# Attention of a diffusion trunk: softmax, weight splits and modulation products in a written order, scale in the queries, one weight queue, gate rows in steps

## The chip, the cores and the metric

The kernel runs on one core of a Trainium2 chip. The metric is the device time of one execution in microseconds, as the median of several runs; lower is better. One further execution is recorded by the profiler, and its rows are what is quoted as the profile and the trace.

Five engines take part. TensorE (PE; its weight loads are listed apart as PEld) multiplies and transposes, VectorE (DVE) and ScalarE (ACT) do the elementwise work and the reductions, GpSimd (POOL) issues a few transfers, and SyncE (SP) issues most of them.

## The reference

One layer on 640 tokens (512 latent, 128 context), D = 1024: a SwiGLU half step, a token mixer, a second half step, each with a normalisation whose shift, scale and gate come from a conditioning vector (`adaln`, nine vectors of 1024 columns). The token mixer projects to ten pieces, runs differential attention beside an mLSTM, gates both and projects back. What the change touches is the attention, the gates of the mLSTM and the modulation columns:

```python
def adaln(cvec, w, b):
    m = jax.nn.silu(cvec) @ w + b
    return m.reshape(cvec.shape[0], N_MOD, D_MODEL)
...
    mq, mk, mv, mo, mg, dq, dk, dv, gm, gd = split_cols(h @ p['w_in'][l])
    dq = rmsnorm(dq.reshape(B, T, DA_HEADS, 2, DA_HEAD_DIM), p['g_qn'][l])
    dk = rmsnorm(dk.reshape(B, T, DA_HEADS, 2, DA_HEAD_DIM), p['g_kn'][l])
...
    # latent tokens: q_att = rope_2d(dq), keys = rope_2d(dk) and 256 cached keys
    scale = DA_HEAD_DIM ** -0.5                      # 64 ** -0.5 = 0.125
    s = jnp.einsum('bqhcd,bkhcd->bhcqk', qi, kf) * scale
    pr = jax.nn.softmax(s, axis=-1)
    w = pr[:, :, 0] - lam * pr[:, :, 1]
    return jnp.einsum('bhqk,bkhv->bqhv', w, vf)
...
    gates = (mg + p['b_gate'][l]) ...
    log_i = gates[:, 0]
    log_f = jax.nn.log_sigmoid(gates[:, 1])          # then running sums and maxima by chunks of 128
```

There are 8 attention heads with two score maps each, over 512 + 256 keys for a latent query and 128 keys for a context query.

## The kernel before

All matmuls of the weights are done with operands split into a high and a low part (`split_w`: ACT copies the raw weights to the high part, DVE subtracts it from the raw weights to give the low part), three products each (`mm3`). Raw weights come into a ring of two buffers (`rawp`, 1 MB each), split weights go to a ring of two (`wp`).

The stage in question is the attention, from line 1464 to line 1670. TensorE's order is written out: every matmul and transpose is kept in program order (`mm`, `tr`). The instructions of DVE, ACT and SP are ordered by the scheduler, from a simulated timeline, unless they pass through `placed` while `as_written` is set or are issued under `issue_after`.

Two streams are woven into each other on TensorE.

- The attention itself, head by head (`Head`, line 1333). A head takes five steps `qi` of 128 queries (four latent, one context). `scores(qi)` makes the score maps of both components (`sc` in PSUM, one buffer), takes the row maxima `mx` on DVE, multiplies them by -0.125 to `nm`, takes two exponentials on ACT with that bias and the scale 0.125 and their row sums `sm`, and mixes the two on DVE: reciprocal `rc`, factor `r`, and the product-sum `p0` (line 1417; the trace names it `p<-p,r,p`). `turn(qi)` transposes `p0` on TensorE (`ps_wT`) and copies the first four blocks to `wT` on ACT, the last two on DVE (line 1432). `values(qi)` multiplies by the values (`ps_o`) and scales by `rc` into `ao`. In the head loop (line 1596) step `qi` does `scores(qi)`, `turn(qi - 1)`, some fill, `values(qi - 1)`, some fill. At `qi == 3` the queries and keys of the next head are packed (`pack`); behind the fifth step they are transposed (`queries`, `keys`, PSUM tile `ps_qkT`).
- The fill (`Fill`, line 1076): the projections by `w_mq`, `w_mk`, `w_dq`, `w_dk`, `w_mv`, `w_dv`, `w_mo`, `w_gm`, `w_gd`, a granule of 256 output columns each, cut into four feature units (`ps_p`, 24 matmuls of 320 columns) or five token units (`ps_t`, 24 matmuls of 256 columns). `slot` runs units as a pace in microseconds asks for. `one` splits the weights of the granule in front and of the one behind it. A granule of `w_dq` or `w_dk` can be held back by `ready` until the last reader of the old queries or keys has been issued. Its last unit is followed by `qk_norm_rope`: normalisation and rotation of 640 tokens, mostly on DVE.

Beside these the stage holds `gate_rows` (line 1176), some 35 small DVE and ACT instructions on the gate logits, written before the first scores; and 14 of the modulation's column products (`Columns.tile`, line 695): a load of 512 KB (`raw_a`), which takes a buffer of the raw weight ring, and two DVE products with a sum (`L704`), in heads 1 to 5. The pools of the mLSTM's queries and keys (`mlq`, `mlk`) are opened before the head loop, when the pool of the gate rows is closed.

Of the kernel before, what the change touches and what calls it, by code (L numbers as in the profile page):

```python
# [7 lines left out]
F32 = mybir.dt.float32  # L8
# [23 lines left out]
def tile_trunk(ctx: ExitStack, tc: tile.TileContext, a: dict):  # L32
# [23 lines left out]


# [74 lines left out]
    def split_into(h, lo, src):  # L132
        raw = load_raw(src)
        act(h, raw, AF.Copy)
        tt(vec, lo, raw, h.bitcast(F32), ALU.subtract)
        return h, lo

    def split_w(src, pool=None, tag="w"):
# [3 lines left out]
        return split_into(h, lo, src)  # L142
# [535 lines left out]
    class Columns:  # L678
# [16 lines left out]
        def tile(self, behind=None):  # L695
# [4 lines left out]
            with ExitStack() as st:  # L700
                if behind is not None:
                    st.enter_context(tc.issue_after(behind.ins))
                for v in range(2):
                    vec.tensor_tensor_reduce(  # L704
                        out=junk, in0=raw, in1=self.csil[:, v, :], op0=ALU.mult, op1=ALU.add, scale=1.0, scalar=0.0,
                        accum_out=mod[:, ct, v : v + 1],
                    )
# [368 lines left out]
    class Fill:  # L1076


        def __init__(self):
            self.q = []  # L1080
            self.due = self.rate = 0.0

        def granule(self, src, units, ready=lambda: True):

            self.q.append([src, units, None, ready])

        def prefetch(self, i):
            if i < len(self.q) and self.q[i][2] is None:
                self.q[i][2] = split_w(self.q[i][0])

        def one(self):
# [4 lines left out]
            self.prefetch(1)  # L1096
# [9 lines left out]
        def blocked(self):  # L1106
            return not self.q or not self.q[0][3]()
# [4 lines left out]
        def slot(self, least=1, weight=1.0):  # L1112
            self.due += self.rate * weight
            while not self.blocked() and (least > 0 or self.due > 1.4):
                self.one()
                least -= 1

        def begin(self, src, units):

            i = 0  # L1120
            while i < len(self.q) and self.q[i][2] is not None:
                i += 1
            w = split_w(src)
            return [lambda u=u: u[1](w) for u in units]
# [51 lines left out]
    def gate_rows(gt, ps):  # L1176
# [16 lines left out]
        stt(lf, fg, 0.0, e, ALU.min, ALU.subtract)  # L1193
# [3 lines left out]
        vec.memset(b, 0.0)  # L1197
        vec.tensor_tensor_scan(out=b[0:4], data0=keep[0:4], data1=lf[0:4], initial=0.0, op0=ALU.mult, op1=ALU.add)
        vec.tensor_tensor_scan(out=b[32:36, ::-1], data0=keep[32:36, ::-1], data1=lf[32:36, ::-1], initial=0.0, op0=ALU.mult, op1=ALU.add)
        tt(vec, u, ig, b, ALU.subtract)  # L1200
# [5 lines left out]
        vec.memset(M, 0.0)  # L1206
        for d0, fl in ((0, False), (32, True)):
            r = slice(d0, d0 + 4)
            for c0, c1, init in ((0, 512, m0[r, 0:1]), (512, 640, 0.0)):
# [3 lines left out]
                vec.tensor_tensor_scan(out=v(M), data0=v(A), data1=v(u), initial=init, op0=ALU.add, op1=ALU.max)  # L1213
        Ml, bl, mn, MP, dc = (gt.tile([64, 5], F32, name=n) for n in ("Ml", "bl", "mn", "MP", "dc"))
# [18 lines left out]

        QA = gt.tile([128, T], F32, name="QA")
# [98 lines left out]
    class Head:  # L1333
# [53 lines left out]
        def scores(self, qi):  # L1387
# [18 lines left out]
            w = 768 if qi < 4 else 128  # L1406
            mx, nm, sm, rc = (ap.tile([128, 2], F32, tag=n, name=n, bufs=2) for n in ("mx", "nm", "sm", "rc"))
            r = ap.tile([128, 1], F32, tag="r", name="r", bufs=2)
            vec.tensor_reduce(out=mx, in_=sv, axis=AX.X, op=ALU.max)
# [7 lines left out]
            stt(p0[:, :w], p1[:, :w], r, p0[:, :w], ALU.mult, ALU.add)  # L1417
            self.s[qi] = (p0, rc)

        def turn(self, qi):  # L1420
# [3 lines left out]
            for k0 in range(0, nk, 4):  # L1424
# [4 lines left out]
                if k0 == 0:  # L1429
                    act(wT[:, :n, :], p[:, :n, :], AF.Copy)  # L1430
                else:
                    vec.tensor_copy(wT[:, k0 : k0 + n, :], p[:, :n, :])
# [48 lines left out]
    g_q, g_k = (load(ap, [128, 64], a[n].partition_broadcast(128), name=n) for n in ("g_qn", "g_kn"))  # L1481
    with tc.issue_after(box["normed"]):
# [54 lines left out]
    with gates:  # L1537
        src_v, e_v = project_v(0)
# [611 lines left out]
```

## Time and profile before

| | us |
|---|---|
| median of 3 runs | 1858.63 |
| lowest and highest | 1857.59, 1860.19 |
| the profiled execution, its own time | 1856.65 |
| its span, first to last instruction | 1854.9 |
| mean granted TensorE clock | 0.994 |

The page lists the busy time of each engine as a share of the span, and groups of instructions as `line engine operation out<-in shape xcount | busy us, mean ns of one | idle time before it and what ended it`. In a list of waits, a row is `who waited <- for whom: us in total, times, longest us`. A line such as L59, L43, L46, L49 or L53 is that of a helper (`mm`, `act`, `tt`, `stt`, `ts`), so groups are told apart by their tiles.

### The profile page before, as it was taken

The numbers are of one execution on the slowest core, as the hardware profiler recorded it, in microseconds if no ns is written. First come the engines' busy times: TensorE is split into PE (matmuls) and PEld (weight loads), VectorE is DVE, ScalarE is ACT, GpSimd is POOL, SyncE is SP. The second block draws the span as 40 slices with busy tenths as digits, with TensorE's granted clock in tenths as the row PEclk, the third lists the DMA queues.
The fourth block names the chain that finished last, engine by engine and source line by source line (L and its number), as shares of the span: only waits on it lengthen the run. The fifth ranks groups of instructions, "written<-read, shape, count | busy, mean of one in ns | idle before, by whom it ended". The sixth has DMA issues, their size and how long they took to land.

```text
span 1854.9 us, 30739 instructions
## 1 busy us (share of the span) xinstructions
PE 1810.4 (98%) x12678; PEld 1771.0 (95%) x12678; DVE 1299.3 (70%) x2181; ACT 834.7 (45%) x1419; POOL 30.9 (2%) x55
## 2 busy tenths in 40 slices
PE   7999999999999999999999999999999999999999
PEld 5999999999999999999999999899999999999999
DVE  5889886586885665765755547874456878887575
ACT  4654544112554353543454346565235645554232
POOL 0000001010000000000000000000000000000000
PEclk9999999999999999999999999999999999999999
DMA  7364457963414322322222254656442345447872
GB/s 288 118 226 161 165 193 277 362 222 132 136 64 130 124 75 95 117 82 96 99 80 75 84 177 144 187 203 215 168 138 94 126 154 177 168 171 258 316 285 85
DMA packets 127901, 299.82 MB, mean 162 GB/s; under 512 B 9553, under 2 KB 90705, under 8 KB 114961
## 3 DMA queue, kind: packets, MB, share of 16 engines
q1 hardware_dynamic: 118498, 257.49, 40.4%
q0 software_dynamic: 9264, 40.37, 5.9%
q8 instruction: 99, 1.62, 0.4%
q14 instruction: 40, 0.33, 0.1%
HBM read 234.20 MB, written 63.63 MB: 161 GB/s over the span
## 4 chain that ended last, share of the span: by engine, by line
PE 83%; DVE 7%; DMA 6%; ACT 2%; issue 1%; SPq 0%; DVEq 0%; ACTq 0%
PE ps_f L59 39%; PE ps_p L59 21%; PE ps_t L59 12%; PE sc L59 2%; PE ps_o L59 2%; DMA ada<-csil_dram 1%; DVE ww L46 1%; PE ps_n L59 1%; PE ps_qkT L62 1%; PE ps_wT L62 1%; DMA raw_a<-in_w_ada_c 1%; DMA raw<-in_w2b 1%; PE ps_u L59 1%; DMA a_raw<-aT_dram 1%; DMA hm<-g_dram 1%
## 5 line engine op out<-in xcount | busy, mean ns | idle before, releaser
L59 PE MATMUL ps_f<-S,ww 128*128 128x320 f32 x1956 | 315.3, 310 | 5.8 <-DVE ww L46 4.0
L59 PEld LDWEIGHTS ps_f<-S,ww 128*128 128x128 f32 x1956 | 294.0, 188 | 8.5 <-DVE ww L46 6.9
L59 PE MATMUL ps_p<-hH,wH 128*128 128x320 f32 x864 | 273.5, 317 | 1.1 <-DVE y L46 0.7
L59 PE MATMUL ps_p<-hH,wL 128*128 128x320 f32 x864 | 267.1, 309 | 0.0
L59 PE MATMUL ps_p<-hL,wH 128*128 128x320 f32 x864 | 267.0, 309 | 0.0
L59 PE MATMUL ps_f<-hm,ww 128*128 128x320 f32 x1236 | 195.0, 310 | 1.5 <-DVE ww L46 1.1
L59 PEld LDWEIGHTS ps_f<-hm,ww 128*128 128x128 f32 x1236 | 185.1, 188 | 2.3 <-DVE ww L46 1.3
L59 PE MATMUL ps_t<-wH,hH 128*128 128x256 f32 x640 | 186.3, 291 | 1.0 <-DVE x L49 1.0
L59 PE MATMUL ps_t<-wH,hL 128*128 128x256 f32 x640 | 182.6, 285 | 0.0
L43 ACT ACTIVATE ww<-raw 128x2048 fp32r<-128x2048 f32 (+1 forms) x61 | 114.1, 1870 | 152.1 <-PE ps_f L59 104.0
L59 PE MATMUL ps_t<-wL,hH 128*128 128x256 f32 x640 | 182.2, 285 | 0.0
L59 PEld LDWEIGHTS ps_p<-hH,wH 128*128 128x128 f32 x864 | 162.4, 188 | 2.5 <-issue 0.9
L59 PEld LDWEIGHTS ps_p<-hL,wH 128*128 128x128 f32 x864 | 162.5, 188 | 0.5
L59 PEld LDWEIGHTS ps_p<-hH,wL 128*128 128x128 f32 x864 | 162.2, 188 | 0.0
L59 PE MATMUL ps_f<-hm,wB 128*128 128x320 f32 x984 | 157.7, 309 | 0.0
L46 DVE TENSOR_TENSOR ww<-raw,ww 128x2048 fp32r<-128x2048 f32 (+1 forms) x61 | 136.4, 2235 | 30.2 <-ACT ww L43 30.2
L59 PEld LDWEIGHTS ps_f<-hm,wB 128*128 128x128 f32 x984 | 147.7, 188 | 0.0
L46 DVE TENSOR_TENSOR wL<-raw,wH 128x2048 fp32r<-128x2048 f32 x49 | 112.1, 2288 | 38.9 <-ACT wH L43 38.8
L43 ACT ACTIVATE wH<-raw 128x2048 fp32r<-128x2048 f32 (+1 forms) x57 | 98.1, 1728 | 88.1 <-PE ps_p L59 83.5
L59 PEld LDWEIGHTS ps_t<-wH,hH 128*128 128x128 f32 x640 | 123.9, 194 | 2.0 <-issue 1.2
L59 PEld LDWEIGHTS ps_t<-wH,hL 128*128 128x128 f32 x640 | 123.8, 193 | 0.5 <-DVE hL L49 0.5
L59 PEld LDWEIGHTS ps_t<-wL,hH 128*128 128x128 f32 x640 | 123.9, 194 | 0.2
(295 smaller groups left out, 3226.7 us busy)
## 6 DMA issues: line engine op xcount, KB each, us to landing
g_dram<-g SPq DMA_DIRECT2D x44, 640.0 KB, 5.5
raw_a<-in_w_ada_c SPq DMA_DIRECT2D x24, 512.0 KB, 4.4
raw<-in_w1b SPq DMA_DIRECT2D x11, 1024.0 KB, 4.8
raw<-in_w3b SPq DMA_DIRECT2D x11, 1024.0 KB, 5.0
raw<-in_w1a SPq DMA_DIRECT2D x10, 1024.0 KB, 4.8
raw<-in_w3a SPq DMA_DIRECT2D x10, 1024.0 KB, 6.1
ada<-in_w_ada_c POOLq DMA_DIRECT2D x18, 512.0 KB, 5.1
hm<-g_dram POOLq DMA_DIRECT2D x7, 1280.0 KB, 10.7
```

The lines of the kernel that those rows point to most:

```text
L43: return placed(nc.scalar.activation(*args, **kw))
L46: return placed(eng.tensor_tensor(out=out, in0=in0, in1=in1, op=op))
L59: tc.keep_in_program_order(nc.tensor.matmul(*args, **kw))
L62: tc.keep_in_program_order(nc.tensor.transpose(*args, **kw))
```

## The change

- **A written order.** A new context `written()` chains the DVE instructions issued under it, and the ACT instructions likewise, to one another in program order, without a semaphore. Instructions outside it are still placed by the scheduler, between or around the chain. Under it stand the reduction of the scores, `turn`, the exponentials (now `soft`), the mix (now a method of its own, after the first fill of the step), `values`, `pack`, the column products in heads 1 to 3 and the splits of `ahead`.
- **The scale.** `g_q` is multiplied by -0.125 once. The row reduction is then a minimum `mn`, used as the bias directly, with the scale -1 in the exponential; `nm` and its product are gone.
- **The transposed weights.** Both copies of `wT` are made by ACT.
- **One weight queue.** All granules are listed at the start, in a fixed order; `w_dq` and `w_dk` of the second pair stand before the first `w_mk`. How many units run at each place is in the table `UNITS`; `ready`, `begin` and the pace are not used in this stage. `ahead()`, at the end of each step, splits the two granules in front and loads the raw weights of the third; `one` splits only the granule in front, if that has not been done.
- **Modulation columns.** The 14 products stand in heads 0 (two) to 3 (four in each of heads 1, 2 and 3). Their loads go to tiles of the `mlq` and `mlk` pools, opened in the third step of head 0 by `begin_pools`.
- **Gate rows.** `gate_rows` is a generator in six pieces; the first runs before head 0, the others over its first three steps (`ROWS`).

```diff
     def placed(ins):
-        if as_written[0]:
+        if as_written[0] is in_row:
+            i = ins.ins
+            if i.engine in in_row:
+                tc.add_manual_dep(
+                    i, in_row[i.engine].name, mybir.DependencyInfo(mybir.DependencyClass.NoSync, mybir.DependencyReason.DATA),
+                    reason="written",
+                )
+            in_row[i.engine] = i
+        elif as_written[0]:
             tc.keep_in_program_order(ins)
         return ins
...
+        def ahead(self):
+            for i in range(2):
+                self.prefetch(i)
+            if len(self.q) > 2 and self.q[2][3] is None:
+                self.q[2][3] = load_raw(self.q[2][0])
...
             self.prefetch(0)
-            self.prefetch(1)
+            if self.eager:
+                self.prefetch(1)
...
-            vec.tensor_reduce(out=mx, in_=sv, axis=AX.X, op=ALU.max)
-            ts(nm, mx, -0.125, ALU.mult)
+            placed(vec.tensor_reduce(out=mn, in_=sv, axis=AX.X, op=ALU.min))
...
+        def soft(self, qi):
...
-                act(p[:, :w], sv[:, c, :], AF.Exp, bias=nm[:, c : c + 1], scale=0.125, accum_out=sm[:, c : c + 1])
-            vec.reciprocal(rc, sm)
+                self.exp = act(p[:, :w], sv[:, c, :], AF.Exp, bias=mn[:, c : c + 1], scale=-1.0, accum_out=sm[:, c : c + 1])
...
+        def mix(self, qi):
+            p0, p1, w, sm, rc = self.s[qi]
+            r = ap.tile([128, 1], F32, tag="r", name="r", bufs=2)
+            placed(vec.reciprocal(rc, sm))
             stt(r, sm[:, 0:1], nlam, rc[:, 1:2], ALU.mult, ALU.mult)
...
-                if k0 == 0:
-                    act(wT[:, :n, :], p[:, :n, :], AF.Copy)
-                else:
-                    vec.tensor_copy(wT[:, k0 : k0 + n, :], p[:, :n, :])
+                act(wT[:, k0 : k0 + n, :], p[:, :n, :], AF.Copy)
...
+    ts(g_q, g_q, -0.125, ALU.mult)
...
+    def begin_pools():
+        gates.close()
+        in_pools["k"] = ctx.enter_context(tc.tile_pool(name="mlk", bufs=1, side="right"))
+        in_pools["q"] = queries_of.enter_context(tc.tile_pool(name="mlq", bufs=1, side="right"))
+        csil = Two(in_pools[t].tile([128, D], F32, tag=t + "3", name="csil") for t in "qk")
+        for v in range(2):
+            nc.sync.dma_start(out=csil[:, v, :], in_=csil_dram[v].partition_broadcast(128))
+        columns.place(14, csil, load_columns, 1)
...
     def load_columns(src):
+        t, junk = (in_pools[p].tile([128, 2, T], F32, tag=p + "2", name="raw_a").rearrange("p a b -> p (a b)") for p in "qk")
+        dma(t[:, :D], src)
+        return t[:, :D], junk[:, : D // 2].bitcast(BF16)
...
+    for pr in range(4):
+        feature(a["w_mq"][pr], lambda pr=pr: q_evac(pr))
+        if pr == 0:
+            token(project_q(1))
+            token(project_k(1))
+        feature(a["w_mk"][pr], lambda pr=pr: k_evac(pr))
+        if pr in (1, 2):
+            token(project_q(pr + 1))
+            token(project_k(pr + 1))
+        rest(pr)
+        if pr < 3:
+            token(project_v(pr + 1))
...
+    ROWS = {(0, 0): 1, (1, 0): 1, (1, 1): 1, (2, 0): 2}
+
+    def aside(hd, qi, part):
+        if hd == 0:
+            for _ in range(ROWS.get((qi, part), 0)):
+                next(rows, None)
+        if part == 0 and (hd in (1, 2, 3) and qi > 0 or hd == 0 and qi > 2):
+            with written():
+                columns.tile()
...
+    UNITS = {
+        0: ((2, 1), (1, 1), (1, 2), (2, 2), (2, 0), (2, 1, 1)), 1: ((2, 1), (1, 1), (1, 1), (1, 1), (1, 0), (1,)),
+        2: ((2, 1), (1, 1), (1, 1), (1, 1), (1, 1), (1, 1, 1)), 3: ((2, 2), (1, 1), (1, 1), (1, 1), (1, 1), (1,)),
+    }
+    UNITS.update({4: UNITS[2], 5: UNITS[3], 6: ((2, 1), (1, 1), (1, 1), (1, 1), (1, 0), (1, 1, 1)), 7: ((2, 1), (1, 1), (1, 1), (1, 0), (1, 0))})
...
         for qi in range(5):
-            if hd or qi:
+            n = UNITS[hd][qi]
+            with written():
                 H.scores(qi)
-            if hd in range(1, 6) and qi in (1, 3) or hd in range(1, 5) and qi == 2:
-                columns.tile()
-            if qi > 0:
-                H.turn(qi - 1)
-            if hd == 1 and qi in (2, 3):
-                gate_cols()
-            fill.slot()
+                if qi > 0:
+                    H.turn(qi - 1)
+                H.soft(qi)
+            aside(hd, qi, 0)
+            fill.units(n[0])
+            with written():
+                H.mix(qi)
...
             if qi > 0:
-                H.values(qi - 1)
+                with written():
+                    H.values(qi - 1)
             if qi == 3 and hd < 7:
-                heads[hd + 1].pack()
-                state["packed"] = hd + 1
-            if qi < 4:
-                fill.slot()
+                with written():
+                    heads[hd + 1].pack()
+            aside(hd, qi, 1)
+            if (hd, qi) == (0, 2):
+                begin_pools()
+            fill.units(n[1])
+            with written():
+                fill.ahead()
```

More of the change, by code (lines that the diff above doesn't have):

```diff
@@ L1 @@
[L1 removed]
+from contextlib import ExitStack, contextmanager
 import concourse.bass as bass
@@ new lines, in tile_trunk @@
+    feature(a["w_gd"][1], lambda: gate_evac(mp, gd_dram, 1))
+    fill.units(2)
+    heads[0].pack_keys()
+    heads[0].queries()
+    fill.units(3)
+    heads[0].keys(0)
+    fill.units(1)
+    heads[0].keys(1)
+    with tc.issue_after(heads[0].at_vec.ins), tc.issue_after(heads[0].at_act.ins):
+        rows = gate_rows(gt, ps_g)
+        next(rows)
+    fill.units(1)
+    fill.eager = False
+    ROWS = {(0, 0): 1, (1, 0): 1, (1, 1): 1, (2, 0): 2}
[6 more added lines that the diff above has]
+                columns.tile()
+        if part == 1 and hd == 1 and qi in (1, 2):
+            gate_load(qi - 1)
+        if part == 0 and hd == 1 and qi in (2, 3):
+            gate_cols()
@@ L1830, in tile_trunk @@
     in_order[0] = False
-    columns.place(10, csil2, load_columns, 1)
-    fill.one()
-    fill.one()
+    columns.place(10, csil2, load_columns_raw, 1)
+    with written():
+        fill.units(2)
     for i in range(5):
```

181 lines of the change are left out of this document (82 added, 99 removed).

## The prediction

> **What bounds the kernel now.** I read the page first, then the table by stretches, then what TensorE waited for, then the chain of waits through one step of the attention.
>
> ```profile
> span 1854.9 us, 30739 instructions
> ...
> PE 1810.4 (98%) x12678; PEld 1771.0 (95%) x12678; DVE 1299.3 (70%) x2181; ACT 834.7 (45%) x1419; POOL 30.9 (2%) x55
> ```
>
> TensorE (PE) is busy for 98% of the span, so nothing but its idle time, and the time in which its clock is down, can be gained: the change leaves every matmul and transpose in place. The edited stage runs from the first score product at 541 us to the last at 1083 us. The next fence is the table by stretches (columns: stretch, its length, busy time of PE, PEld, DVE, ACT and POOL with instruction counts, granted clock, DMA share, GB/s).
>
> ```profile
> 541.00:1083.00 542.00, 530.12 (x4078) 520.99 (x4077) 345.47 (x568) 241.49 (x468) 0.00 (x0) 1.00 0.29 96
> 541.00:618.00 77.00, 72.30 (x514) 70.52 (x513) 51.69 (x92) 30.40 (x59) 0.00 (x0) 1.00 0.37 120
> 533.00:536.40 3.40, 3.40 (x19) 3.40 (x18) 3.25 (x9) 2.84 (x5) 0.00 (x0) 0.50 0.00 0
> 672.90:676.30 3.40, 3.40 (x22) 3.40 (x20) 1.98 (x3) 2.63 (x5) 0.00 (x0) 0.51 0.02 5
> ```
>
> PE idles 542 - 530.1 = 11.9 us in the stage, and in two stretches of 3.4 us its clock is at half, which loses 1.7 us each. DVE (345 of 542, 64%) and ACT (45%) have room on average. So the stage is bound by PE, broken by a few waits. These are the waits of the weight loads from 520 to 1083 us, and the one wait of PE itself that lies ahead of 541:
>
> ```profile
> PEld ps_wT L62 <- DVE p L49: 7.6, 6, 2.2
> PEld ps_o L59 <- DVE wT L1432: 3.2, 2, 2.2
> PEld ps_qkT L62 <- issue: 2.7, 1, 2.7
> PEld ps_qkT L62 <- ACT kpk L43: 1.9, 1, 1.9
> ```
> ```profile
> PE ps_qkT L62 <- ACT kpk L43: 1.7, 1, 1.7
> ```
>
> Ten waits, 7.6 + 3.2 + 2.7 + 1.9 = 15.4 us by the weight loads; by PE's own idle time 11.9 + 1.7 = 13.6. I take the middle, 14.5.
>
> **How a wait comes about.** DVE from 838 to 847 us, and the transpose that it held up:
>
> ```profile
> 838.06 2.28 DVE L46 TENSOR_TENSOR wL<-raw,wH 128x2048 fp32r<-128x2048 f32 x1
> 840.25 0.16 DVE L53 TENSOR_SCALAR nm<-mx 128x2 f32<-128x2 f32 x1
> ...
> 844.91 1.23 DVE L704 CUSTOM_DVE_ANT_0 raw_a<-raw_a,csil 128x1024 bf16<-128x1024 f32 x1 [1.41 <-DMA raw_a<-in_w_ada_c]
> ...
> 846.07 1.01 DVE L49 SCALAR_TENSOR_TENSOR p<-p,r,p 128x768 f32<-128x768 f32 x1
> ```
> ```profile
> 847.14 0.55 PE L62 MATMUL ps_wT<-ident,p 128*128 128x128 f32 x3 [1.81 <-DVE p L49]
> ```
>
> Between the maximum and its tiny product nm the scheduler put a weight split (2.28), so the exponentials, which need nm, started that much late. Then a modulation product, itself waiting 1.41 for its DMA, went ahead of the mix of the two softmaxes (line 1417), and the transposes waited 1.81 for that. The work was not too much; its order was wrong.
>
> **The change, part by part.** First the cover of one step, from the chain in order of time, and a feature unit from elsewhere in the chain (columns: start, us, what):
>
> ```profile
> 627.51 1.41 PE sc L59 x8
> 628.92 0.66 PE ps_wT L62 x6
> 629.58 2.87 PE ps_t L59 x24
> 632.45 1.34 PE ps_o L59 x12
> ```
> ```profile
> 710.00 3.52 PE ps_p L59 x24
> ```
>
> From the end of one score product PE has the transposes of the step before (0.66), a unit, the values (1.34), a second unit and the next scores (1.41) to do before it needs the mix: 0.66 + 2.87 + 1.34 + 2.87 + 1.41 = 9.15 us with token units, 10.45 with feature units. What must fit in comes from the groups of instructions of the stage (count | busy us, mean ns of one | idle before):
>
> ```profile
> L46 DVE TENSOR_TENSOR wL<-raw,wH 128x2048 fp32r<-128x2048 f32 x28 | 64.0, 2287 | 12.6 <-ACT wH L43 12.5
> L1409 DVE TENSOR_REDUCE mx<-sc 128x2 f32<-128x1536 f32 x32 | 56.2, 1756 | 40.1 <-PE sc L59 40.0
> L704 DVE CUSTOM_DVE_ANT_0 raw_a<-raw_a,csil 128x1024 bf16<-128x1024 f32 x28 | 34.2, 1223 | 20.6 <-DMA raw_a<-in_w_ada_c 15.0 <-DMA csil<-csil_dram 5.4
> L49 DVE SCALAR_TENSOR_TENSOR p<-p,r,p 128x768 f32<-128x768 f32 x32 | 32.6, 1017 | 0.9
> L1432 DVE COPY wT<-ps_wT 128x256 f32<-128x256 f32 x32 | 13.3, 416 | 0.1
> L49 DVE SCALAR_TENSOR_TENSOR r<-sm,nlam,rc 128x1 f32<-128x1 f32 x40 | 8.8, 219 | 1.1
> L53 DVE TENSOR_SCALAR nm<-mx 128x2 f32<-128x2 f32 x40 | 6.5, 162 | 0.3
> L1272 DVE TENSOR_REDUCE ss<-sq 128x20 f32<-128x1280 f32 x6 | 8.9, 1479 | 0.0
> ```
> ```profile
> L43 ACT ACTIVATE p<-sc,nm 128x768 f32<-128x768 f32 x64 | 57.1, 900 | 37.0 <-DVE nm L53 32.4 <-DVE bl L1216 4.6
> L43 ACT ACTIVATE wH<-raw 128x2048 fp32r<-128x2048 f32 x27 | 51.6, 1911 | 42.0 <-PE ps_p L59 42.0
> L43 ACT ACTIVATE stage<-ps_t 128x256 f32<-128x256 f32 x20 | 7.7, 383 | 22.6 <-PE ps_t L59 22.1 <-ACT p L43 0.5
> ```
>
> *Scale folded.* The 40 nm products go (6.5 us of DVE). The reduction becomes a minimum of the same shape, so 1.76 as before, and nothing can stand between it and the exponentials any more. The one new product, on 64 columns of g_q, has no reason to differ from a small DVE product; beside matmuls I price it at 0.
>
> *Transposed weights.* The 32 second copies leave DVE (13.3 us) for ACT, at 0.383 each by a copy of the same size out of PSUM: 12.3 us more on ACT, 47% instead of 45%. They follow the first copy at once and have a unit of PE work for cover. The two waits of ps_o for wT on DVE (3.2) go; what is late next is the first copy, already on ACT.
>
> *Written order.* Reduction 1.76, two exponentials 1.80, then reciprocal (about 0.16, as nm), r 0.22, mix 1.02: 5.0 us against 9.15. With a modulation pair behind the reduction (2 x 1.22) the exponentials run beside it: 1.76 + 2.45 + 1.40 = 5.6, slack 3.5. The worst place is a split whose buffer has only just come free: ACT half 1.91, then DVE half 2.29 ahead of the reduction. That ends 4.2 us after the unit instead of the 1.41 of the scores, 2.8 later: 8.4 of 9.15. It still fits, by under 1 us, once each in heads 3 and 5. Splits elsewhere come a unit or more after their buffer is free. So the six waits for p (7.6) should go.
>
> *Projection order.* The granules for heads 2 and 3 move ahead of the keys of the first mLSTM head, so the rotation of q_tok ends about a granule earlier (4 x 3.52 = 14 us), and the wait of 2.7 at 672 us goes, with the half clock behind it (1.7). One more unit (2.87) ahead of the first key transposes covers the 1.9 of kpk; the other half clock (1.7) goes with it. Gain of the clock: 3.4.
>
> A rule weighed: the Trainium skill, page "TensorE: Matmul & The Clock Gate", section "What's actually happening", says that the clock halves after an idle window of about 3.4 us. By that page neither wait here would do it, and the sum would be 3.4 us smaller. The trace disagrees with a full window as the condition: half-clock stretches follow waits of 1.7 and 2.7 us. But it also shows 1.00 over 541 to 618 us, where PE idled 77 - 72.3 = 4.7 us, so not each wait brings one.
>
> *Gate rows and columns.* The same DVE work, in five pieces over head 0, where up to two units stand on either side. The modulation products move from heads 1 to 5 into heads 0 to 3, into memory that comes free when the gate rows have left by DMA in the third step; the weight ring no longer shares its two buffers with them. I allow 1 us of new wait there (bounds 0 and 3).
>
> *What is left or new.* The rotations are not in the written chain: six sets with a reduction of 1.48 and several passes like it can still slip in ahead of a reduction or mix. With a slack of 3.5 in the usual step one passes free; in the tight steps it shows. Bounds 0 and 6 x 2 passes x 1 us = 12, and I take 3, a quarter. One more for steps with a single unit. Sum of new waits 1 + 3 + 1 = 5, bounds 0 and 15.
>
> Sum: -14.5 - 3.4 + 5 = -12.9 us. The profiled execution took 1856.65 (span 1854.9), 1.98 below the median 1858.63 of the three runs; on the median the forecast is 1845.7.
>
> **Rivals.**
>
> *The written order waits for its own DMA (slower).* On DVE the modulation pair now stands between reduction and mix, whatever its data does. The load for it is issued by SP after the pair before has ended:
>
> ```profile
> raw_a<-in_w_ada_c SPq DMA_DIRECT2D x14, 512.0 KB, 4.2
> ```
> ```profile
> SPq L81 <- DVE wL L46: 109.9, 12, 18.1
> ```
>
> It lands 4.2 us after issue, and the next pair is a step (9.15) later, so SP may be held 9.15 - 4.2 = 4.95 us at no cost, and 3.5 more eat the slack. Beyond a hold of 8.45 us PE waits. SP's waits for splits average 109.9 / 12 = 9.2 us. If twelve loads were held 11 us, the price would be 12 x 2.5 = 30: 1858.6 - 17.9 + 30 = 1871. Against it: the load has a buffer of its own now, and SP waits that long because it is early. The Trainium skill, page "PSUM — Partial Sum Buffer", section "Engine vs sequencer instructions", says that the queues of ScalarE and VectorE are strict FIFO; by that rule a fixed order makes this worse than before. The trace agrees: at 844.91 the product that waited held the mix behind it.
>
> *The waits only move (no change).* If the rotations and splits, now fitted around a rigid chain, cost 0.45 us in each of 40 steps, that is 18 us, and the time stays at 1858.7. For it: DVE keeps about 60% load. Against: the slack of 3.5.
>
> *Half of it.* With 9 to 14 us of new waits, near the upper bounds: 1849.7 to 1854.7.
>
> *Everything is covered.* No new waits: 1840.7, or 1839.8 with 15.4 for the waits.
>
> **How the numbers follow.** A measurement tells about 0.2%, 3.7 us, from no change. Forecast (new waits 0.5 to 9) 0.55; everything covered 0.08; half of it 0.15; waits only move 0.10; slower by the DMA wait or another stop of the chain 0.12. Faster 0.55 + 0.08 + 0.15 = 0.78, same 0.10, slower 0.12. The range goes from 1838, which is 1839.8 less the spread of the runs, to 1857, which leaves out the slower case and most of the case of moved waits, just under 0.2.
>
> **What would show it.** Right: no nm group; no wL and no modulation product between reduction and exponential; the rows of PEld waiting for p and for wT under 3 us together; clock 1.00 through 520 to 1083; idle PE there under 6 us. Wrong: DVE waiting for raw_a by more than 15 us in the stage, with the transposes waiting for p behind it; the transposes of queries waiting for qpk; a half-clock stretch in a new place; or an idle TensorE after 1083, where I expect nothing.

## The result, and the profile after

| | before | after |
|---|---|---|
| median, us | 1858.68 (4 runs, 1857.59 to 1860.19) | 1838.37 (4 runs, 1836.26 to 1840.01) |
| ratio, 95% interval | | 0.989 (0.9872 to 0.9907) |
| the profiled execution, its span | 1856.65, 1854.9 | 1838.32, 1836.5 |
| mean granted clock | 0.994 | 0.998 |

The change makes the kernel 20.3 us faster (1.1%), inside the range (1838 to 1857), by 0.4 us, and 7.3 below the predicted 1845.7. In the two profiles the spans differ by 18.4 us; the other 1.9 is that the profiled execution before lay 2 us under its median and the one after lies on it.

From the page of the kernel after:

```profile
PE 1802.6 (98%) x12678; PEld 1764.6 (96%) x12678; DVE 1282.8 (70%) x2110; ACT 844.2 (46%) x1451; POOL 30.9 (2%) x55
```

TensorE has the same 12678 matmuls, DVE 71 instructions fewer and ACT 32 more. The table by stretches of the kernel after, with the columns of before:

```profile
480.00:541.00 61.00, 61.00 (x482) 59.63 (x482) 48.35 (x93) 34.87 (x66) 0.00 (x0) 1.00 0.36 121
541.00:1083.00 542.00, 537.79 (x4150) 529.83 (x4149) 333.26 (x506) 256.29 (x507) 0.00 (x0) 1.00 0.29 97
```

PE idles 542 - 537.8 = 4.2 us where it idled 11.9, does 72 matmuls more in the same time, and has its full clock throughout; in the 61 us ahead of it, where the wait of 1.7 with its half clock stood, it does not idle at all. What it still waits for from 520 to 1083 us, by PE and by its weight loads (of these the rows for ps_wT):

```profile
PE ps_wT L78 <- DVE p L57: 3.5, 3, 1.7
PE ps_p L75 <- ACT aT L51: 0.7, 1, 0.7
```
```profile
PEld ps_wT L78 <- DVE p L57: 3.3, 2, 2.2
PEld ps_wT L78 <- PE sc L75: 1.3, 1, 1.3
```

Where ten waits stood there are now three for the mix, and one of 0.7 behind the last scores. The groups of the stage show what the chain of DVE consists of now (from 535 to 1070 us):

```profile
L1430 DVE TENSOR_REDUCE mn<-sc 128x2 f32<-128x1536 f32 x32 | 56.1, 1754 | 62.0 <-PE sc L75 61.8
L720 DVE CUSTOM_DVE_ANT_0 raw_a<-raw_a,csil 128x1024 bf16<-128x1024 f32 x28 | 34.1, 1217 | 2.0 <-DMA raw_a<-in_w_ada_c 1.8
L51 ACT ACTIVATE wT<-ps_wT 128x256 f32<-128x256 f32 x32 | 12.1, 379 | 0.0
```

The reduction now waits for scores (62.0 us of idle before it, 40.1 before the change): DVE is ahead of TensorE, as it should be. The column products wait 2.0 us where they waited 20.6.

**Where the 18.4 us come from.** TensorE's order is written out and the matmuls are the same, so a stage can be timed between two matmuls that mean the same in each kernel. The next table is worked out from the start times of these matmuls in the traces of all kernels of this study. *Start*: up to the last product of the gate logits. *Attention*: from there to the last score product. *End*: to the first key transpose of the mLSTM. *mLSTM*: to its last output product (`ps_n`). *Rest*: to the last matmul.

| kernel | start | attention | end | mLSTM | rest |
|---|---|---|---|---|---|
| before | 517.4 | 555.96 | 24.10 | 153.58 | 599.84 |
| after | 517.6 | 541.20 | 25.04 | 149.23 | 599.37 |
| order not written | 519.5 | 556.65 | 24.10 | 154.28 | 599.24 |
| before, with the relief | 520.0 | 556.02 | 24.10 | 155.15 | 599.25 |
| product and copy back | 521.4 | 551.67 | 25.04 | 148.40 | 599.46 |
| product back | 517.5 | 547.28 | 25.03 | 148.62 | 598.98 |
| copy back | 518.3 | 542.80 | 25.05 | 148.14 | 598.78 |
| old granule order | 521.9 | 550.54 | 24.11 | 150.56 | 598.77 |
| columns in the ring | 520.4 | 541.31 | 25.04 | 147.30 | 598.82 |
| unit of the prelude back | 519.8 | 541.87 | 25.05 | 149.53 | 599.33 |
| end not written | 520.0 | 540.93 | 26.59 | 153.35 | 599.96 |
| rows held | 519.6 | 538.41 | 25.05 | 148.58 | 598.94 |
| rows held, columns moved | 519.8 | 537.15 | 25.04 | 148.04 | 598.79 |

Attention gives 14.8, the end takes 0.9, the mLSTM gives 4.35, and the rest 0.5. The start, which no kernel changes, differs by up to 4.5 us between executions, and one execution stands behind each row; that is why the experiments below are read by their stages first and by their medians second. How far a stage can be trusted: three kernels whose attention should be alike (after, columns in the ring, end not written) lie between 540.9 and 541.3, but a half-clock stretch that falls in one execution and not in another moves a stage by 1.7.

**The three waits that are left.** At 555 us, ahead of the first mix of head 0; DVE of the kernel after:

```profile
546.48 1.76 DVE L1430 TENSOR_REDUCE mn<-sc 128x2 f32<-128x1536 f32 x1
...
550.44 2.58 DVE L1234 TENSOR_TENSOR_SCAN lf<-keep,m,u 4x512 f32<-4x512 f32 x2
...
555.98 1.00 DVE L57 SCALAR_TENSOR_TENSOR p<-p,r,p 128x768 f32<-128x768 f32 x1
```

The scan is part of the gate rows. These rows are written in pieces over head 0, but no instruction ties a piece to its step: the scheduler put nearly all of them around the first reduction and ahead of the first mix. It is the wait that before had at the same place (1.73 here, 1.74 there). At 774 us, DVE in the second step of head 3:

```profile
766.21 2.29 DVE L54 TENSOR_TENSOR wL<-raw,wH 128x2048 fp32r<-128x2048 f32 x1 [1.27 <-ACT wH L51]
768.42 1.75 DVE L1430 TENSOR_REDUCE mn<-sc 128x2 f32<-128x1536 f32 x1
...
771.23 1.48 DVE L1295 TENSOR_REDUCE ss<-sq 128x20 f32<-128x1280 f32 x1
...
774.21 1.02 DVE L57 SCALAR_TENSOR_TENSOR p<-p,r,p 128x768 f32<-128x768 f32 x1
```

This is the worst place of the prediction: a split whose buffer has just come free stands ahead of the reduction, the step fits by under 1 us, and a pass of the rotation (1.48), which is not in the chain, slips in between the two column products of the step. TensorE is held 0.88. The third, 0.93 at 666 us, is the slower rival's mechanism, once:

```profile
663.85 1.23 DVE L720 CUSTOM_DVE_ANT_0 raw_a<-raw_a,csil 128x1024 bf16<-128x1024 f32 x1 [1.24 <-DMA raw_a<-in_w_ada_c]
```

The mix of that step waits behind this product.

### The profile page after: what moved, and what is told of

The parts are those of the page before. It is cut to its first block, busy times and chain, and to the rows that moved or that the text cites. A ratio compares the mean times of both kernels' runs of the same rounds, so it can differ in the third digit from the quotient of the medians.

```text
span 1836.5 us, 30726 instructions
## 1 busy us (share of the span) xinstructions
PE 1802.6 (98%) x12678; PEld 1764.6 (96%) x12678; DVE 1282.8 (70%) x2110; ACT 844.2 (46%) x1451; POOL 30.9 (2%) x55
## 4 chain that ended last, share of the span: by engine, by line
PE 83%; DVE 7%; DMA 6%; ACT 2%; issue 1%; SPq 0%; DVEq 0%; ACTq 0%
PE ps_f L75 40%; PE ps_p L75 22%; PE ps_t L75 12%; PE sc L75 2%; PE ps_o L75 2%; DMA ada<-csil_dram 1%; DVE ww L54 1%; PE ps_n L75 1%; DMA raw_a<-in_w_ada_k 1%; PE ps_wT L78 1%; PE ps_qkT L78 1%; DMA raw<-in_w3a 1%; DVE raw_a L720 1%; DMA P<-nm_dram 1%; PE ps_u L75 1%
## 5 line engine op out<-in xcount | busy, mean ns | idle before, releaser
L54 DVE TENSOR_TENSOR raw<-raw 128x1024 f32<-128x1024 f32 x141 | 121.7, 863 | 1.8
## 6 DMA issues: line engine op xcount, KB each, us to landing
hm<-g_dram POOLq DMA_DIRECT2D x7, 1280.0 KB, 10.5
```

The costliest lines, as they stand in the source:

```text
L54: return placed(eng.tensor_tensor(out=out, in0=in0, in1=in1, op=op))
```

## Experiments

Eleven kernels ran. "Order", in the first three expectations, is the theory that the written order brings the gain, "relief" that taking work off DVE brings it.

### The order not written

The whole change, but `written()` leaves the placing to the scheduler.

```diff
-        was, as_written[0] = as_written[0], in_row
+        was = as_written[0]
```

> The changed kernel with the chain of the written order taken off; everything else (scale in the queries, copies on ACT, granule order, units, columns, gate rows) stays. Theory ORDER (the waits of TensorE came from the order in which DVE and ACT took their work): waits of the transposes for p come back, five or more of them, 6 to 10 us: 1844 to 1849. Theory RELIEF (the 20 us less of DVE work took the waits away): within 2 us of the changed kernel, 1837 to 1840. Theory PLACEMENT (where units and granules stand did it): the same as RELIEF, 1837 to 1840.

Measured: 1860.26 (1857.93 to 1862.99, 10 runs), ratio to before 1.0013 (1.0004 to 1.0022). All of the gain is gone, in the attention (+15.5 against after) and in the mLSTM (+5.1). DVE of this kernel at 640 us, and the transpose that waited for it:

```profile
639.95 0.22 DVE L57 SCALAR_TENSOR_TENSOR r<-sm,nlam,rc 128x1 f32<-128x1 f32 x1
640.08 2.29 DVE L54 TENSOR_TENSOR wL<-raw,wH 128x2048 fp32r<-128x2048 f32 x1
642.28 1.22 DVE L54 TENSOR_TENSOR q_tok<-q_tok,sw 128x1024 f32<-128x1024 f32 x1
...
645.29 1.01 DVE L57 SCALAR_TENSOR_TENSOR p<-p,r,p 128x768 f32<-128x768 f32 x1
```
```profile
646.45 0.88 PE L78 MATMUL ps_wT<-ident,p 128*128 128x128 f32 x3 [4.75 <-DVE p L57]
```

The factor r was ready, and a split and passes of the rotation went ahead of the mix that was one instruction away: 5.1 us. Without the order, the relief and the new arrangement are worth nothing. It is a bigger loss than the order theory had said.

### Before, with the relief alone

The kernel before with the scale folded into `g_q` (minimum as bias, no nm) and both `wT` copies on ACT; all else as before.

```diff
-            vec.tensor_reduce(out=mx, in_=sv, axis=AX.X, op=ALU.max)
-            ts(nm, mx, -0.125, ALU.mult)
+            vec.tensor_reduce(out=mn, in_=sv, axis=AX.X, op=ALU.min)
...
-                if k0 == 0:
-                    act(wT[:, :n, :], p[:, :n, :], AF.Copy)
-                else:
-                    vec.tensor_copy(wT[:, k0 : k0 + n, :], p[:, :n, :])
+                act(wT[:, k0 : k0 + n, :], p[:, :n, :], AF.Copy)
...
+    ts(g_q, g_q, -0.125, ALU.mult)
```

> The kernel before with nothing but the scale folded into the queries (no nm product) and both copies of the transposed weights on ACT. ORDER: only the two waits of ps_o for wT (3.2 us) go, the waits for p stay at about 7: 1853 to 1857. RELIEF: most of the gain in the attention, 10 us or more: 1848 or less.

Measured: 1860.29 (1856.82 to 1863.96, 10 runs), ratio 1.0011 (0.9999 to 1.0022): no gain. Its longest waits from 520 to 1083 us:

```profile
PE ps_wT L62 <- DVE p L49: 4.2, 3, 2.0
PE ps_qkT L62 <- DVE qpk L46: 3.7, 1, 3.7
PE ps_wT L62 <- DVE rt L49: 2.9, 1, 2.9
```

The waits for `wT` on DVE are gone, as they must be; those for qpk and for rt (a part of the rotation) have grown in their place. By the start times in the traces, over the 40 steps the exponentials now start 11.3 us in all after the end of their reductions, where it was 72.9; but from the reciprocal to the mix, which the scheduler can still fill, it is 33.2 us, where it was 25.6. Taking 20 us of work off DVE moved the waits and freed nothing: both theories had expected some gain.

### After, with product and copy back on DVE

The reverse of that: the whole change, but the maximum with its small product and the second `wT` copy are on DVE again, in the written order (the exponential scales by 0.125, and `g_q` is left alone).

```diff
-            placed(vec.tensor_reduce(out=mn, in_=sv, axis=AX.X, op=ALU.min))
+            placed(vec.tensor_reduce(out=mx, in_=sv, axis=AX.X, op=ALU.max))
+            ts(mn, mx, -0.125, ALU.mult)
...
-                act(wT[:, k0 : k0 + n, :], p[:, :n, :], AF.Copy)
+                if k0 == 0:
+                    act(wT[:, :n, :], p[:, :n, :], AF.Copy)
+                else:
+                    placed(vec.tensor_copy(wT[:, k0 : k0 + n, :], p[:, :n, :]))
```

> The changed kernel with the 40 nm products and the 32 second copies put back on DVE, both in the written chain. ORDER: the chain of a step is longer by 0.16 and the copy of 0.42, under the slack of 3.5 in most steps; up to two more small waits: 1838 to 1842. RELIEF: 8 to 10 us come back: 1846 to 1849.

Measured: 1851.54 (1849.14 to 1854.98, 6 runs), ratio 0.9968 (0.9956 to 0.998). The attention takes 10.5 us more than after (in this execution the start was 3.8 longer as well). So the order theory falls too, and it is more than the relief theory had (1849 at most): with the order, the relief is worth 10 us in these two traces, 3.4 of it two half-clock stretches; without the order, nothing. The place in head 3 again:

```profile
775.50 1.75 DVE L1430 TENSOR_REDUCE mx<-sc 128x2 f32<-128x1536 f32 x1
777.17 1.48 DVE L1295 TENSOR_REDUCE ss<-sq 128x20 f32<-128x1280 f32 x1
778.56 0.16 DVE L61 TENSOR_SCALAR mn<-mx 128x2 f32<-128x2 f32 x1
778.63 0.42 DVE L1462 COPY wT<-ps_wT 128x256 f32<-128x256 f32 x1
```

The written order says what follows what, not that nothing comes between. Between reduction and product there is a crack, the rotation's pass (1.48) went into it, and the copy, written behind the product, was late for the values (2.25 us of wait). The next two runs take the two halves alone.

### The copy back alone

The second half of that diff.

> The changed kernel with only the 32 second copies of the transposed weights back on DVE, in the written chain; the scale stays folded. With copies and nm products both back the values waited 6.4 us for the copy, which stood behind a split, the reduction, a rotation pass and nm. Theory COPY (the copy's place in the chain is the price): those waits stay, with the reduction still ahead: 1844 to 1849. Theory CRACK (the nm product is the price, since the scheduler puts other work between the reduction and it): within 2 us of the changed kernel, 1837 to 1841.

Measured: 1840.87 (1838.86 to 1844.59, 4 runs), ratio 0.9915 (0.9895 to 0.9934); attention +1.6, inside what the theory of the crack gave. The values wait for the copy in three places:

```profile
PE ps_o L75 <- DVE wT L1461: 2.1, 3, 0.8
```

The price of the two together must come from the product or from the pair.

### The product back alone

Its first half.

> Undoes the folded scale alone: the row reduction is a maximum again, followed by the small DVE product with -0.125 (in the written order), and the exponential scales by 0.125. Both copies of the transposed weights stay on ACT. Theory CRACK (the price of putting the work back, 10.5 us of attention, is carried by the small product: it opens a place between reduction and exponential into which the scheduler puts gate rows, splits or rotation passes): 1845 to 1850, attention 548 to 552 us, and the waits of the transposes for the mix 8 us or more. Theory SUM (neither product nor copy costs much alone; it takes both, since only a late exponential and a DVE copy together hold up the values): 1838 to 1842, attention under 544.

Measured: 1845.85 (1843.58 to 1848.67, 4 runs), ratio 0.9942 (0.9925 to 0.9959); attention 547.28, +6.1. The time is the one that the crack theory gave, the waits for the mix are 6.0 and not 8, and the stage ends just below its 548. The product alone costs 6.1, the copy alone 1.6, both 10.5. Half-clock stretches make 1.7, 0 and 3.4 of these, so that the pair costs 7.1 without them and the halves 4.4 and 1.6: whether the two together cost more than their sum is not shown. What TensorE waits for here from 520 to 1083 us on account of the softmax, and then DVE in head 0, where the first of the two long waits comes from the crack:

```profile
PE ps_wT L78 <- DVE p L57: 6.0, 3, 3.5
PE sc L75 <- ACT p L51: 1.0, 2, 0.5
```

```profile
546.34 1.76 DVE L1430 TENSOR_REDUCE mx<-sc 128x2 f32<-128x1536 f32 x1
548.12 0.49 DVE L1259 COPY QA<-u 64x640 f32<-64x640 f32 x1
...
550.30 0.17 DVE L61 TENSOR_SCALAR mn<-mx 128x2 f32<-128x2 f32 x1
...
557.60 1.00 DVE L57 SCALAR_TENSOR_TENSOR p<-p,r,p 128x768 f32<-128x768 f32 x1
```

2.2 us of gate rows stand between the end of the reduction (548.1) and the product, and TensorE waits 3.50 where after waits 1.73. Twice more, in heads 3 and 5, a pass of the rotation is in the crack and the next scores wait 0.5 for the exponentials to leave `sc`. So the crack is seen in many steps (over the 40, the exponentials start 26.3 us in all after their reductions end; in after it is 4.8), but it is shown to cost TensorE 2.8 us. The other long wait, 2.19 at 786 us, comes from four passes of the rotation between reciprocal and mix, an opening that after has as well; with the half clock behind it, it makes 3.9 of the 6.1. That it was used here and not there I can only put down to a schedule that came out otherwise, so the number that the crack theory gave is reached in part by another way.

### The old order of granules

```diff
+        feature(a["w_mk"][pr], lambda pr=pr: k_evac(pr))
         if pr in (1, 2):
             token(project_q(pr + 1))
             token(project_k(pr + 1))
-        feature(a["w_mk"][pr], lambda pr=pr: k_evac(pr))
```

> Undoes the projection order alone: the granule of w_mk stands ahead of those of w_dq and w_dk for the second and third pair of heads, as before the change. Theory of the prediction (that order brought the wait of the query transposes, 2.7, and the half clock behind it, 1.7): that wait returns after head 1, the time is 1841 to 1845. Theory ORDER-MADE (the rotation of q_tok was late because of what DVE had been given ahead of it, and is in time in the new order either way): no such wait, 1837 to 1840.

Measured: 1850.89 (1847.8 to 1851.62, 6 runs), ratio 0.9966 (0.9954 to 0.9977); attention +9.3. The wait returns behind head 1, as expected, but three times as long and at another tile, and the time is above what either theory gave. ACT, TensorE, and the table by stretches of this kernel there:

```profile
675.07 1.36 ACT L51 ACTIVATE kpk<-k_tok 128x640 fp32r<-128x640 f32 x2 [4.94 <-DVE k_tok L54]
676.34 0.85 ACT L51 ACTIVATE wT<-ps_wT 128x512 f32<-128x512 f32 x2
```
```profile
676.96 1.01 PE L75 MATMUL ps_o<-v_tok,wT 128*128 128x128 f32 x3 [7.97 <-ACT wT L51]
```
```profile
672.10:682.30 10.20, 5.34 (x28) 5.34 (x29) 6.04 (x13) 4.47 (x12) 0.00 (x0) 0.50 0.17 54
```

In the written order of ACT the packing of the next head's keys (kpk) stands ahead of the `wT` copy. It waits 4.94 for the rotation, and everything written behind it waits too: the values 8 us, and the clock is at half for 10.2, from within the wait on (TensorE is busy for 5.34 of them, so this costs some 2.7). The written order has turned a late input, which cost 2.7 + 1.7 before, into 9.3. The order of granules is no extra: the written order needs it.

### The columns in the weight ring

```diff
-        t, junk = (in_pools[p].tile([128, 2, T], F32, tag=p + "2", name="raw_a").rearrange("p a b -> p (a b)") for p in "qk")
+        t = rawp.tile([128, 2048], F32, tag="raw", name="raw_a")
         dma(t[:, :D], src)
-        return t[:, :D], junk[:, : D // 2].bitcast(BF16)
+        return t[:, :D], t[:, D : D + D // 2].bitcast(BF16)
```

> The column products load into the ring of two raw weight buffers, as before the change, and not into memory of their own; their order on DVE stays written. Theory of the slower rival (a fixed order waits for its own DMA once the loads share the ring: a load is held until a split has ended, a step of 9 us or more): 12 loads held 2 to 11 us too long, 1850 to 1871, with DVE waiting for raw_a by over 15 us and the transposes waiting for the mix behind it. Theory NO-HOLD (each step's splits free a buffer before the load is due): 1837 to 1842.

Measured: 1838.66 (1837.82 to 1841.54, 4 runs), ratio 0.9906 (0.9888 to 0.9925): the same as after. The products in this kernel, from 541 to 1083 us:

```profile
L720 DVE CUSTOM_DVE_ANT_0 raw_a<-raw_a,csil 128x1024 bf16<-128x1024 f32 x28 | 34.1, 1218 | 2.2 <-DMA raw_a<-in_w_ada_c 2.0
```

2.2 us of wait against 2.0. The slower rival's mechanism finds no room here even with the shared ring; what took away the 20.6 of before is the order and not the memory. The kernel with the order not written says the same from the other side: there the products have memory of their own and their new places, and DVE waits 25.8 us before them.

### One unit of the prelude back

Two units instead of three ahead of the first keys, and one more behind the second.

```diff
-    fill.units(3)
+    fill.units(2)
...
-    fill.units(1)
+    fill.units(2)
```

> The changed kernel with two units instead of three ahead of the first key transposes, and one more behind the second. Prediction's step: the unit covers the wait of 1.9 for kpk, and the half clock behind it (1.7): 1840 to 1842. If the clock does not halve: 1839.5 to 1841. If the cover was not needed: 1837 to 1839.

Measured: 1840.64 (1839.55 to 1845.91, 4 runs), ratio 0.9917 (0.9893 to 0.9941). Waits and table by stretches of this kernel:

```profile
PE ps_qkT L78 <- ACT kpk L51: 1.7, 1, 1.7
PE ps_wT L78 <- DVE p L57: 0.9, 1, 0.9
```
```profile
535.40:538.80 3.40, 3.40 (x18) 3.40 (x18) 2.80 (x8) 2.91 (x5) 0.00 (x0) 0.50 0.00 0
```

Both come back together, the wait and the half clock. From the last gate product to the first score product it is 27.62 us against 24.17: 3.45, as 1.9 + 1.7 had it. The attention as a whole shows only 0.7 of that, because the waits at 555 and 666 us are not in this trace; the wait of head 3 (0.88) is. The medians differ by 2.3.

### The end not written

`H.finish` of the last head, and the two units ahead of the mLSTM, outside the written order. (The list of the change does not name these two places, nor the two column products of head 0; all stand in the written order as well.)

```diff
-            with written():
-                H.finish()
+            H.finish()
...
-    with written():
-        fill.units(2)
+    fill.units(2)
```

> The changed kernel with the two places behind the last head (the last head's transposes of its output with their copies, and the first two units after it with their split) taken out of the written order. The mLSTM stage lost 4.4 us in the changed kernel, which no part of the prediction named. Theory END (ACT now copies the last output before the next split, so SP issues the mLSTM's first loads 2.7 us earlier after the last transposes): the wait of 3 us and the half clock return: 1841 to 1844. Theory CHANCE (the schedule of that stage moved for other reasons): 1837 to 1840.

Measured: 1845.81 (1844.36 to 1846.7, 4 runs), ratio 0.9938 (0.9923 to 0.9953). End +1.55, mLSTM +4.1: the gain behind the attention is that of these two lines, and without them the time is above what the theory had (1844). ACT and then SP in the kernel before, and the same after:

```profile
1089.91 1.92 ACT L43 ACTIVATE wH<-raw 128x2048 fp32r<-128x2048 f32 x1 [2.93 <-PE ps_p L59]
...
1092.04 0.94 ACT L43 ACTIVATE aT<-ps_aT,gs 128x512 f32<-128x512 f32 x2
```
```profile
1093.01 0.32 SPq L1461 DMA_DIRECT2D aT_dram<-aT  x1
...
1095.03 0.99 SPq L81 DMA_DIRECT2D P<-nm_dram  x2
```
```profile
1075.98 0.95 ACT L51 ACTIVATE aT<-ps_aT,gs 128x512 f32<-128x512 f32 x2
1076.81 1.91 ACT L51 ACTIVATE wH<-raw 128x2048 fp32r<-128x2048 f32 x1
```
```profile
1076.95 0.32 SPq L1487 DMA_DIRECT2D aT_dram<-aT  x1
...
1077.80 1.16 SPq L97 DMA_DIRECT2D P<-nm_dram  x2
```

Before, ACT split weights first and then finished the attention's output (aT); SP stores that output and only behind it loads P. After, aT goes first. The mLSTM's first score products (`ps_st`) run without P, until one of them needs a PSUM buffer: it comes free behind the work on P, in before by a copy (`stage`) that stands on ACT behind the exponentials of P, in after by the product with P itself. The first product that waits, before and after:

```profile
1103.14 0.58 PE L59 MATMUL ps_st<-mqT,mkT 128*128 128x128 f32 x1 [3.33 <-ACT stage L43]
```
```profile
1087.32 0.71 PE L75 MATMUL ps_st<-mqT,mkT 128*128 128x128 f32 x4 [1.08 <-DVE P L54]
```

3.33 of wait, with a half-clock stretch behind it (1.7), against 1.08: 3.95 of the 4.35.

### Rows held, and columns moved

The later pieces of the gate rows are issued behind the mix of the step before them. In a second kernel two column products are also moved, from the step (head, `qi`) = (1, 4) to (2, 0) and from (3, 1) to (3, 0), where DVE has more room.

```diff
-    ROWS = {(0, 0): 1, (1, 0): 1, (1, 1): 1, (2, 0): 2}
+    ROWS = {(0, 1): 1, (1, 0): 1, (1, 1): 1, (2, 0): 2}
...
-                next(rows, None)
+                with tc.issue_after(heads[0].mixed.ins):
+                    next(rows, None)
```

> The changed kernel with the later pieces of the gate rows bound behind the mix of the step before them (the second piece one place later). The trace of the changed kernel shows 3.4 us of gate row work on DVE ahead of the first reduction and 4 us between it and the mix, and a wait of 1.9 us at 555. If that work is what delays the mix, the wait goes: 1836 to 1837, and no new one. If the rows are then late for the pools that open behind them in the third step, a wait of 1 to 4 us appears near 570 to 590 instead: 1838 to 1841.

> The changed kernel with the gate rows bound behind the mix, as measured, and two modulation products moved: from the last step of head 1 to the first of head 2, and from the second step of head 3, where a split has just come free, to its first. If the wait of 1.0 at 774 came from the product standing in the tight step, it goes: 1 us below the kernel with the rows bound alone, 1834 to 1836. If the rotation pass alone makes it, it stays or moves by a step: 1835 to 1838.

Measured: 1835.87 (1833.86 to 1838.9, 4 runs), ratio 0.9882 (0.9865 to 0.9899), and with the columns 1834.74 (1834.54 to 1834.95, 4 runs), 0.9879 (0.9865 to 0.9894). The attention falls by 2.8 and by 1.3 more. Of the 2.8, 1.95 is the wait at 555 us, which the held rows end. The rest is the wait at 666 us: there DVE does the same work in the same order, and the load of the column product took 1 us less to land; that wait is missing, too, in kernels whose rows are not held (the copy back, the unit of the prelude back). In the second kernel the wait at 774 us is gone as well, though the rotation's pass still stands between reduction and mix, so it took the pass and the column products together. No wait for a mix is left; the table by stretches:

```profile
541.00:1083.00 542.00, 541.33 (x4180) 533.98 (x4179) 336.63 (x513) 258.63 (x516) 0.00 (x0) 1.00 0.30 99
```

PE idles 0.7 us in the stage. This is the best version of the study, 3.6 us below the change by the medians; the intervals of the ratios overlap, but each of its four runs lies below each of the four of the change, and the stages say where the difference is.

## Why the prediction was right, and where it fell short

The sum was -14.5 (waits), -3.4 (clock), +5 (new waits). The attention gave 14.8, so by the stage the waits that remain or are new come to 14.5 + 3.4 - 14.8 = 3.1, within 0.5 to 9 and under the 5 taken; by PE's own idle time the three waits for the mix are 3.5. (The 1083 us that the prediction gives as the last score product is the last product by the values; the last scores stand at 1073. The terms do not change by it.)

The mechanism was right, the number less so. The median lies below the 1841 to 1850 that new waits of 0.5 to 9 would give, and even below the rival in which everything is covered (1839.8 to 1840.7), though not everything is covered: 3.4 us came from behind the attention, where nothing was forecast, and 1.9 from where the profiled execution lay. That the time is still inside the range, by 0.4, is luck.

- **Scale folded.** That nothing can stand between reduction and exponential any more was the right reading; priced through the waits for p it was right in kind. The run with the product back puts 6.1 us on it, of which 2.8 is seen to come out of that opening.
- **Transposed weights.** The 3.2 of ps_o are gone; the copy back brings 1.6. ACT's copies took 12.1 us, 12.3 was forecast.
- **Written order.** Five of the six waits for p are gone, and two of 0.9 are new. The worst place was named with its heads and showed in head 3, by the rotation that was allowed for, on top of the column products; head 5 has none.
- **Projection order.** The wait and the half clock (4.4) went as said. What they cost without that order was undersized: 9.3, since the written order carries the hold on to the copies behind it.
- **Prelude.** 1.9 + 1.7 forecast, 3.45 measured at the place; over the attention as a whole 0.7.
- **Gate rows.** This step failed. I allowed for them as spread "in five pieces over head 0"; the trace shows them unspread, and the old wait at 555 us where it was. Writing a piece later does not place it later. Holding the pieces is worth 1.95, the whole of that wait.
- **The end.** "An idle TensorE after 1083, where I expect nothing": the two stages behind the attention became 3.4 us shorter (4.35 less 0.9), and I had not followed `H.finish` through ACT and SP to the load of P. This is the larger part of the missing 5.5 us of span; 1.9 is the new waits, and the median's place adds 1.9.
- **The marks.** No nm group, the clock at 1.00, and 4.2 us of idle time (under 6) came as said; the weight loads' waits for p and wT are 3.3, just over the 3. Nothing long stands between a reduction and its exponentials: in all 40 steps they start at most 0.8 us after its end, by the start times in the trace.
- **The rivals.** The wait for its own DMA exists, once, for 1.24 us. That waits only move is what the relief alone did, in the old order.

Which of order and relief brings the gain has no answer by parts: the order without the relief (product and copy back, but with the new arrangement of granules, units and columns) keeps 4.3 of the attention's 14.8, the relief alone keeps none, and both together all of it. The written order in the old arrangement was not run; the old order of granules alone, under the written order, costs 9.3. Nor was the table `UNITS` changed by itself.

## What to carry to other kernels

When an engine that is two thirds busy makes the bound engine wait, look at what stands ahead of the instruction it waits for before taking work off: here 20 us less work alone gave nothing. A written order fixes a sequence but leaves cracks between its members, and hands on each late input to all that is written behind it; so close the cracks on the short path (here, by dropping the tiny product between two long steps), and see to it that what feeds the row is early. Work that should run later must be tied to something late; writing it later is not enough.

## What the hardware showed

The half-clock stretches, which the prediction could not sort, sort by a grid. In each trace all of them begin at one phase of a period of 3.41 us (before: 92.7, 533.0, 672.9, 1103.0 are 129, 41 and 126 periods apart), another phase in each execution. What decides is how much TensorE idles within one such window. Windows of the kernel before, two by two, each with the one behind it:

```profile
669.50:672.90 3.40, 0.95 (x10) 0.74 (x9) 3.40 (x5) 1.04 (x3) 0.00 (x0) 1.00 0.23 77
672.90:676.30 3.40, 3.40 (x22) 3.40 (x20) 1.98 (x3) 2.63 (x5) 0.00 (x0) 0.51 0.02 5
843.60:847.00 3.40, 1.73 (x11) 1.21 (x9) 2.08 (x4) 0.44 (x1) 0.00 (x0) 1.00 0.42 136
847.00:850.40 3.40, 3.26 (x24) 3.27 (x25) 3.30 (x6) 0.66 (x2) 0.00 (x0) 1.00 0.48 129
```

2.45 us idle, and the next window runs at half; 1.67 idle, and it does not. Over the thirteen traces, from 341 to 1800 us, half clock followed 19 of 19 full-clock windows with more than 1.85 us idle, 3 of 15 with 1.6 to 1.85, and none of 50 with 0.8 to 1.6. So the border is near half a window, and a long wait can escape: the 3.50 us wait in the kernel with the product back was cut by the grid into 1.69 and 1.81, and the clock stayed full. The same wait of 3.50 in the kernel with product and copy back fell nearly whole into one window (3.39 idle), and the next ran at half. The Trainium skill, page "TensorE: Matmul & The Clock Gate", section "What's actually happening", gives a free-running window of 3413 ns, and the traces agree; it says that the clock falls after an idle window, and there the traces decide otherwise: a window a little more than half idle is enough. In these traces idle time of under 1.6 us within a window cost only itself; between 1.6 and 1.85 the clock fell now and then (so behind the 1.7 for kpk, in before and with the unit of the prelude back); above 1.85 it always fell, which costs 1.7 more. Whether a longer wait puts that much into one window depends on the phase that the execution happens to have. That may be a source of the scatter between runs of one kernel; no run here separates it from others.
